# A TensorE order written out by hand while the modulation comes in by quarters, in a one-core diffusion block

## The chip, the cores and the metric

The kernel runs on one core of one Trainium2 chip. The metric is the device time of one execution in microseconds (us). Three runs of the kernel before took 872.28, 872.78 and 876.59 us, with a median of 872.78 us.

## What is computed

One layer on 1024 latent tokens and 256 context tokens of width 1024. What matters here is its beginning:

```
shift, scale, gate = split(silu(c) @ w_ada + b_ada, 3)       # c: 1024, w_ada: 1024 x 3072
h  = rmsnorm(x, g_pre) * (1 + scale) + shift                  # 1024 x 1024
hc = rmsnorm(ctx, g_pre) * (1 + scale_c) + shift_c            # 256 x 1024, from c_ctx
na_q, na_k, na_v, na_z, g_qkv, g_z, g_b, g_a = split(h @ w_in)   # w_in: 1024 x 4112
...
x + gate * rmsnorm(concat([o_na * silu(na_z), o_g * silu(g_z)]) @ w_out, g_post)
```

Neighbourhood attention and a bidirectional gated delta rule follow; they fill the rest of the time and are not touched.

## The kernel before, in words

The code in question is `phase0`, the first 110 us or so. The features of h are its 1024 input channels, in eight slices of 128 (k = 0 to 7) that stand on the partitions. Everything is needed as a pair of fp32r tiles, a high part and the rest: `hh` and `hl` for h, `wh` and `wl` for weights. A product is then three matmuls: hh with wh, hl with wh, hh with wl.

**Shift and scale by quarters.** `ada(q)` (line 287) handles slices 2q and 2q+1. It loads four pieces of w_ada of 512 KB (tiles `wada`, seven buffers), multiplies each with two matmuls of 32 columns (`par`, line 294), and loads and splits two groups of weights (`wr_nv`, `wr_qk`: a cast on ScalarE at line 448, a subtraction on GpSimd at line 449). Then VectorE copies the sums (`rows`, line 306), four small matmuls turn them (`pa`, line 310), VectorE makes `ab` and `am` (lines 314 and 315), and `modulate` (line 255) makes hh and hl of both slices: VectorE at line 259, ScalarE at line 265, VectorE at line 266.

**Products of a quarter.** `products(q)` (line 323) adds slices 2q and 2q+1 to six sums in PSUM for the first 512 tokens (group 0): `pv` of four token tiles (24 matmuls of 264 columns) and `pq`, `pk` (12 matmuls of 512 columns). The code calls `ada(q)` and then `products(q-1)` (lines 353 to 356).

**Group 1.** The other 512 tokens come as rows (`xra`, four loads), whose squares ScalarE sums (line 337), and transposed (`xta`, four loads into the same four buffers, so each waits for a square). The norms go through GpSimd, VectorE, a transpose on TensorE (`prr`, line 245) and a copy on ScalarE (`rbb`, line 246). Two gate products for group 0 (`pz`, 24 matmuls of 512 columns each, with the weights `wg1536` and `wg3584`) are called between the groups.

**What sets the order.** All loads are issued on SyncE's queue (SP) in the order of the code (`chain`), each one after the buffer that it fills is free; the raw weights `wr` have three buffers. The order on the five engines is set by the framework's scheduler, which puts an instruction where its own timing model finds it ready. A hand-made edge (`order`) ties one instruction behind another on its engine without a wait on the chip. Before the change there is one such edge for TensorE in this stage: the first `pq` matmul of products(2) stands behind the last `pa` matmul of quarter 3 (`self.after`, lines 328 and 464). `pe` (line 594), used later in the kernel, ties each TensorE instruction that it is given behind the one given before.

Of the kernel before, what the change touches and what calls it, by code (L numbers as in the profile page):

```python
# [20 lines left out]
P = 128  # L21
# [120 lines left out]
class K:  # L142
    def __init__(self, tc, I, out, dbg=None):
        self.tc, self.nc, self.I, self.out = tc, tc.nc, I, out
        self.dbg = dbg or {}
        self.na_first = None
        self.gm = {}
        self.gate = self.after = None

    def order(self, r, before):  # L150
        self.tc.add_manual_dep(r.ins, before, mybir.DependencyInfo(mybir.DependencyClass.NoSync,
                               mybir.DependencyReason.DATA), reason="order on a queue")

# [40 lines left out]
    def phase0(self):  # L194
# [10 lines left out]
        with tc.tile_pool(name="p0", bufs=1, side="right", reuse_waits="tile") as p0:  # L205
# [50 lines left out]
            def modulate(rw, hi, lo, k, w, rb, alt=True):  # L256
                m = hi.shape[-1]
                a, b = am[:, k, w:w + 1], ab[k // 2][:, 0, k % 2, w:w + 1]
                nc.vector.scalar_tensor_tensor(rw, rw, a, rb[:, :m], ALU.mult, ALU.mult)
                if k % 2 and alt:  # L260
                    nc.scalar.activation(rw, rw, AF.Identity, bias=b)
                    nc.scalar.copy(hi, rw)
                    nc.gpsimd.tensor_tensor(lo, rw, hi.bitcast(F32), ALU.subtract)
                else:
                    nc.scalar.activation(hi, rw, AF.Identity, bias=b)  # L265
                    nc.vector.scalar_tensor_tensor(lo, rw, b, hi.bitcast(F32), ALU.add, ALU.subtract)
# [18 lines left out]
            sels = []  # L285

            def ada(q):
                par = at(f"par{q}", "tb", 2)
                for k2 in range(0, KC, 2):
                    wa = p0.tile([P, 2, 2, 256], F32, name=f"wada{q}{k2}", tag="wada", bufs=7)  # L290
                    chain(wa, I["w_ada"][q][:, k2:k2 + 2])
                    for j in range(2):
                        g = 32 * ((k2 + j) % 4)
                        nc.tensor.matmul(par[g:g + 32, :], sc[:, k2 + j, :],
                                         wa[:, j, :, :].rearrange("p n c -> p (n c)"),
                                         start=(k2 < 4), stop=(k2 >= 4), tile_position=(0, g))
# [9 lines left out]
                nc.vector.tensor_copy(rows, par)  # L306
                pa = at(f"pa{q}", "tb", 2)[:, :8].rearrange("p (n c w) -> p n c w", n=2, c=2)
                for n in range(2):
                    for cc in range(2):
                        last = nc.tensor.matmul(pa[:, n, cc, :], rows[:, 256 * n + P * cc:256 * n + P * cc + P],  # L310
                                                self.sel, start=True, stop=True).ins.name
# [7 lines left out]
                sels.append(last)  # L319
# [3 lines left out]
            def products(q):  # L323
                ks = range(2 * q, 2 * q + 2)
                for t in g0:
                    self.mm_tok(pvs[t][:, :264], wv, 0, 264, self.nat_tok(t - 2), ks)
                for i in range(2):
                    if i == 0 and q + 1 in (3,):
                        self.after = sels[q + 1]
# [22 lines left out]

            for q in range(4):
                ada(q)
                if q:
                    products(q - 1)
# [9 lines left out]
            products(3)  # L366
# [67 lines left out]
    def load_w(self, pool, c0, n, tag, bufs=(3, 4, 4), halves=2, load=None, ks=None, dst=None):  # L434
# [5 lines left out]
        for k0 in [ks[0]] if ks else range(0, KC, kk):  # L440
# [7 lines left out]
            nc.scalar.copy(hi, raw)  # L448
# [6 lines left out]
    def mm_chan(self, ps, w, hh, hl, t0, n, perm=False, ks=range(KC)):  # L455
        nc = self.nc
        his, los = w
        for k in ks:
# [4 lines left out]
            r = nc.tensor.matmul(ps, wh, xh, start=(k == 0), stop=False)  # L463
            if self.after:
                self.order(r, self.after)
                self.after = None
            nc.tensor.matmul(ps, wh, xl, start=False, stop=False)  # L467
            nc.tensor.matmul(ps, wl, xh, start=False, stop=(k == KC - 1))  # L468

    def mm_tok(self, ps, w, c0, n, xsel, ks=range(KC)):  # L470
        nc = self.nc
        his, los = w
        for k in ks:
            wh, wl = his[k][:, c0:c0 + n], los[k][:, c0:c0 + n]
            xh, xl = xsel(k)
            nc.tensor.matmul(ps, xh, wh, start=(k == 0), stop=False)  # L476
            nc.tensor.matmul(ps, xl, wh, start=False, stop=False)  # L477
            nc.tensor.matmul(ps, xh, wl, start=False, stop=(k == KC - 1))  # L478
# [1078 lines left out]
```

## Time and profile before

| | us |
|---|---|
| median of three runs | 872.78 |
| the profiled execution | 871.71 |
| its span | 869.9 |
| TensorE busy in the span | 824.9 (95%) |
| VectorE, ScalarE, GpSimd busy | 502.7, 417.3, 357.3 |
| mean granted TensorE clock | 0.972 of 2.4 GHz |

A busy time is the sum in which an engine has an instruction under way. A share over the whole span mixes stages; the stage of the change is read from the timeline. "PEclk" is the clock that TensorE was granted, as a share of 2.4 GHz; 0.50 is 1.2 GHz. TensorE's matmuls overlap, so what one costs in a dense stretch is the distance from its start to the next one's start, which is shorter than the duration in the row.

### The profile page before, as it was taken

The numbers are of one execution on the slowest core, as the hardware profiler recorded it, in microseconds if no ns is written. First come the engines' busy times: TensorE is split into PE (matmuls) and PEld (weight loads), VectorE is DVE, ScalarE is ACT, GpSimd is POOL, SyncE is SP. The second block draws the span as 40 slices with busy tenths as digits, with TensorE's granted clock in tenths as the row PEclk, the third lists the DMA queues.
The fourth block names the chain that finished last, engine by engine and source line by source line (L and its number), as shares of the span: only waits on it lengthen the run. The fifth ranks groups of instructions, "written<-read, shape, count | busy, mean of one in ns | idle before, by whom it ended". The sixth has DMA issues, their size and how long they took to land.

```text
span 869.9 us, 16461 instructions
## 1 busy us (share of the span) xinstructions
PE 824.9 (95%) x6082; PEld 696.4 (80%) x6082; DVE 502.7 (58%) x1051; ACT 417.3 (48%) x1087; POOL 357.3 (41%) x430
## 2 busy tenths in 40 slices
PE   6999999999999989989898999899999999999996
PEld 3678887888788867769786788788898988878885
DVE  3444455536743699859935964456666655653342
ACT  5244334753664643355314334366666667734210
POOL 2224141453462553328262100655757559624110
PEclk9999999999999999989998999699999999999999
DMA  8778352255444825562597569995967925134251
GB/s 340 265 259 295 97 170 88 73 170 168 142 157 154 221 85 170 176 171 81 176 283 226 160 187 290 419 258 149 313 179 262 259 78 191 49 110 133 87 184 69
DMA packets 86054, 159.65 MB, mean 184 GB/s; under 512 B 18373, under 2 KB 45334, under 8 KB 83798
## 3 DMA queue, kind: packets, MB, share of 16 engines
q1 hardware_dynamic: 78486, 144.94, 53.0%
q10 hardware_dynamic: 7488, 13.67, 5.1%
q8 instruction: 48, 0.79, 0.4%
q14 instruction: 32, 0.26, 0.1%
HBM read 109.51 MB, written 52.42 MB: 186 GB/s over the span
## 4 chain that ended last, share of the span: by engine, by line
PE 59%; DVE 16%; DMA 15%; issue 4%; ACT 2%; POOL 2%; SPq 1%; DVEq 0%; POOLq 0%; ACTq 0%
PE py L1369 3%; PE py L1370 3%; PE py L1371 3%; DVE tb L1078 3%; DVE vb L1081 3%; PE pa L1260 2%; PE pz L463 2%; PE pz L468 2%; PE pz L467 2%; PE po L789 2%; DMA wada<-in_w_ada 2%; PE pa L1271 2%; PE po L784 2%; DMA pm_dram<-pm 2%; PE tr L772 2%
## 5 line engine op out<-in xcount | busy, mean ns | idle before, releaser
L759 ACT ACTIVATE pt<-pt,nm 128x544 f32<-128x544 f32 (+1 forms) x64 | 50.5, 790 | 37.5 <-DVE nm L758 37.0
L758 DVE CUSTOM_DVE_ANT_0 pt<-sc,gm 128x544 f32<-128x544 f32 (+1 forms) x64 | 49.4, 771 | 32.2 <-PE sc L754 25.8
L742 POOL TENSOR_TENSOR gm<-gt,mk 128x288 f32<-128x288 f32 (+1 forms) x48 | 46.5, 971 | 29.1 <-DVE nm L758 28.8
L1232 POOL TENSOR_SCALAR kd<-kt,kd 128x128 f32<-128x128 f32 x72 | 42.7, 605 | 20.5 <-PE pa L1271 19.9
L1020 ACT ACTIVATE em<-em,gc 128x128 f32<-128x128 f32 x80 | 25.5, 391 | 34.9 <-DMA em<-gc_dram 29.7
L467 PE MATMUL pz<-hl,wh_gz 128*128 128x512 f32 x96 | 38.6, 402 | 0.0
L463 PE MATMUL pz<-hh,wh_gz 128*128 128x512 f32 x96 | 38.3, 399 | 0.0
L468 PE MATMUL pz<-hh,wl_gz 128*128 128x512 f32 x96 | 38.2, 398 | 0.0
L476 PE MATMUL pv<-wh_nv,hh 128*128 128x264 f32 x128 | 35.5, 296 | 2.0 <-ACT hh L265 1.7
L477 PE MATMUL pv<-wh_nv,hl 128*128 128x264 f32 x128 | 36.8, 292 | 0.0
L1431 DVE TENSOR_TENSOR finv<-py,ggb 128x512 f32<-128x512 f32 x16 | 10.9, 689 | 43.2 <-ACT finv L1430 43.1
L478 PE MATMUL pv<-wl_nv,hh 128*128 128x264 f32 x128 | 35.6, 287 | 0.0
L1274 DVE SCALAR_TENSOR_TENSOR s<-s,egl,pa 128x128 f32<-128x128 f32 x64 | 19.6, 344 | 27.2 <-PE pa L1271 27.2
L1039 POOL TENSOR_SCALAR_AFFINE_SELECT qe<-qe 128x256 f32<-128x256 f32 x32 | 25.5, 800 | 24.1 <-DVE qe L1038 24.1
L887 DVE SCALAR_TENSOR_TENSOR acc_v<-xp_v,cols,acc_v 128x1282 f32<-128x1282 f32 x16 | 29.1, 1817 | 10.9 <-ACT acc_v L885 10.6
L1078 DVE TENSOR_TENSOR tb<-ab,vb 120x31 f32<-120x31 f32 (+15 forms) x62 | 30.2, 487 | 8.7 <-DMA ab<-ab_dram 7.1
L1137 POOL COPY tm<-ld 32x320 f32<-32x320 f32 x16 | 7.4, 464 | 65.0 <-DMA tm_dram<-tm 27.1
L1430 ACT ACTIVATE finv<-py 128x512 f32<-128x512 f32 x16 | 9.5, 597 | 48.6 <-PE py L1371 30.5
L1238 POOL TENSOR_SCALAR vb<-v,beta 128x128 f32<-128x128 f32 x40 | 24.2, 604 | 20.4 <-DVE y L1244 17.2
L772 PE MATMUL tr<-c,pt 128*96 128x128 f32 (+1 forms) x192 | 31.8, 275 | 0.0
L1035 DVE SCALAR_TENSOR_TENSOR pm<-pk,beta,em 128x128 f32<-128x128 f32 x80 | 23.5, 342 | 14.0 <-PE pk L1028 10.9
L770 ACT COPY tcx<-tc 128x256 f32<-128x256 f32 x64 | 23.4, 366 | 16.2 <-PE tc L768 15.8
(432 smaller groups left out, 2852.7 us busy)
## 6 DMA issues: line engine op xcount, KB each, us to landing
wada<-in_w_ada SPq DMA_DIRECT2D x16, 512.0 KB
em<-gc_dram SPq DMA_DIRECT2D x20, 256.0 KB
pm_dram<-pm SPq DMA_DIRECT2D x20, 256.0 KB
tm_dram<-tm SPq DMA_DIRECT2D x8, 640.0 KB
kk<-qk_dram SPq DMA_DIRECT2D x16, 320.0 KB
tm<-tm_dram SPq DMA_DIRECT2D x4, 1280.0 KB
kq_dram<-kq SPq DMA_DIRECT2D x4, 1152.0 KB
kq<-kq_dram SPq DMA_DIRECT2D x4, 1152.0 KB
```

What stands on the lines that cost most here:

```text
L463: r = nc.tensor.matmul(ps, wh, xh, start=(k == 0), stop=False)
L467: nc.tensor.matmul(ps, wh, xl, start=False, stop=False)
L468: nc.tensor.matmul(ps, wl, xh, start=False, stop=(k == KC - 1))
L476: nc.tensor.matmul(ps, xh, wh, start=(k == 0), stop=False)
L477: nc.tensor.matmul(ps, xl, wh, start=False, stop=False)
L478: nc.tensor.matmul(ps, xh, wl, start=False, stop=(k == KC - 1))
L742: r = nc.gpsimd.tensor_tensor(self.gm[hh][:, 384 - n:384].rearrange("p (n c r) -> p n c r", c=nco, r=4), gv, self.mk[:, mo:mo + n].rearran ...
L758: nc.vector.tensor_tensor_reduce(pt[:, 384 - n:], sc[:, 512 - n:768], gm[:, 384 - n:], -1.0, 3.0e38, ALU.add, ALU.min, nm)
L759: self.last_exp = nc.scalar.activation(pt[:, 384 - n:], pt[:, 384 - n:], AF.Exp, bias=nm, scale=-1.0, accum_out=sums[:, ct, hh:hh + 1]).in ...
L772: self.pe(nc.tensor.transpose(pl[:m, rc * P:(rc + 1) * P], pt[:, 384 + (rc - 3) * m:384 + (rc - 2) * m], self.ident))
L1078: nc.vector.tensor_tensor(t3, bc(ab[:, 0:m, m:m + 1], [r, m, n]), bc(vb[:, m:m + 1, m:], [r, m, n]), ALU.mult)
L1232: r = nc.gpsimd.tensor_scalar(kd[d], kt_[:, t, :], self.kd[:, h, d, t:t + 1], None, ALU.mult)
```

## The change

Every TensorE instruction issued between the start of quarter 0 and the end of products(2), and again in products(3), is tied behind the one before in the order of the code (`mm` calls `pe` while `seq` is set). `ada` and `products` become generators, so that the code can be interleaved: `ada(q)` stops after the copy `rows`, `products(q)` after two and after four token tiles. The order of the code in quarter q is then: pv of tiles 2 and 3 for quarter q-1; the eight `par` matmuls of quarter q; pv of tiles 4 and 5 for quarter q-1; `pa` of quarter q; pq and pk for quarter q-1. On ScalarE the weight casts of a quarter, and the squares in `load_rows`, are tied behind the last hh that was issued before them in the code.

```diff
+    def mm(self, *a, **k):
+        r = self.nc.tensor.matmul(*a, **k)
+        if self.seq:
+            self.pe(r)
...
-                    nc.scalar.activation(hi, rw, AF.Identity, bias=b)
+                    self.last_hh = nc.scalar.activation(hi, rw, AF.Identity, bias=b).ins.name
...
                 rows = p0.tile([P, 512], F32, name=f"rows{q}", tag="rows", bufs=1)
                 nc.vector.tensor_copy(rows, par)
+                yield
                 pa = at(f"pa{q}", "tb", 2)[:, :8].rearrange("p (n c w) -> p n c w", n=2, c=2)
...
             def products(q):
                 ks = range(2 * q, 2 * q + 2)
                 for t in g0:
                     self.mm_tok(pvs[t][:, :264], wv, 0, 264, self.nat_tok(t - 2), ks)
+                    if t % 2:
+                        yield
                 for i in range(2):
-                    if i == 0 and q + 1 in (3,):
-                        self.after = sels[q + 1]
                     self.mm_qk(pqk[i], wqk[i], i, 0, ks)
...
-                    nc.scalar.activation(x, x, AF.Square, accum_out=ss[:, i:i + 1])
+                    self.order(nc.scalar.activation(x, x, AF.Square, accum_out=ss[:, i:i + 1]), self.last_hh)
...
+            self.seq = True
+            before = iter(())
             for q in range(4):
-                ada(q)
-                if q:
-                    products(q - 1)
+                a = ada(q)
+                for g in (before, a, before, a, before):
+                    next(g, None)
+                before = products(q)
+            self.seq = False
...
-            products(3)
+            self.seq = True
+            for _ in before:
+                pass
+            self.seq = False
...
-            nc.scalar.copy(hi, raw)
+            r = nc.scalar.copy(hi, raw)
+            if self.seq and self.last_hh:
+                self.order(r, self.last_hh)
```

The matmuls of `ada`, `mm_chan` and `mm_tok` go through `self.mm`; `self.after` and `sels` are gone. No instruction is added, removed or resized. The built programs differ in order on all engines within the first 440 of TensorE's instructions, and nowhere after.

The first place is TensorE around the `par` matmuls of quarter 1 (`par1<-wada10` to `wada16`; `pv2_1` to `pv5_1` are the four token tiles, `wh_nv10_0` the weights of slices 0 and 1). Before:

```order
L310 MATMUL pa0_250<-c128_60,rows0_248 128x2 x4
L294 MATMUL par1_264<-wada10_265,sc_129 32x512 x2
L476 MATMUL pv2_1_204<-wh_nv10_0_228,hh_112 128x264
L476 MATMUL pv3_1_205<-wh_nv10_0_228,hh_112 128x264
L476 MATMUL pv4_1_206<-wh_nv10_0_228,hh_112 128x264
L476 MATMUL pv5_1_207<-wh_nv10_0_228,hh_112 128x264
L463 MATMUL pq0_0_208<-hh_112,wqk_h_202 128x512
L463 MATMUL pk0_0_209<-hh_112,wqk_h_202 128x512
L294 MATMUL par1_264<-wada12_269,sc_129 32x512 x2
```

After, from the end of the pv matmuls of tiles 2 and 3:

```order
L157 MATMUL pv3_1_205<-wh_nv10_0_228,hl_113 128x264
L157 MATMUL pv3_1_205<-wl_nv10_0_229,hh_112 128x264
L157 MATMUL par1_276<-wada10_277,sc_129 32x512 x2
L157 MATMUL par1_276<-wada12_281,sc_129 32x512 x2
L157 MATMUL par1_276<-wada14_285,sc_129 32x512 x2
L157 MATMUL par1_276<-wada16_289,sc_129 32x512 x2
L157 MATMUL pv4_1_206<-wh_nv10_0_228,hh_112 128x264
L157 MATMUL pv4_1_206<-wh_nv10_0_228,hl_113 128x264
```

Before, the four pairs of quarter 1 stand apart, the first ahead of any product and the others among them; now they stand in a row behind the twelve matmuls of tiles 2 and 3.

The second place is ScalarE at the modulation of quarter 3 (`hh<-raw,ab3`). Before:

```order
L448 CAST wg1536h_501<-wr_gz15360_0_503 128x512
L448 CAST wg1536h_501<-wr_gz15364_4_507 128x512
L337 ACTIVATE xra0_513,ss4__511<-xra0_513 128x1024
L337 ACTIVATE xra1_516,ss4__511<-xra1_516 128x1024
L265 ACTIVATE hh_112<-raw_135,ab3_456 128x512 x2
L337 ACTIVATE xra2_519,ss4__511<-xra2_519 128x1024
L337 ACTIVATE xra3_522,ss4__511<-xra3_522 128x1024
```

After:

```order
L461 CAST wg1536h_501<-wr_gz15360_0_503 128x512
L461 CAST wg1536h_501<-wr_gz15364_4_507 128x512
L272 ACTIVATE hh_112<-raw_135,ab3_480 128x512 x2
L342 ACTIVATE xra0_513,ss4__511<-xra0_513 128x1024
L342 ACTIVATE xra1_516,ss4__511<-xra1_516 128x1024
L342 ACTIVATE xra2_519,ss4__511<-xra2_519 128x1024
L342 ACTIVATE xra3_522,ss4__511<-xra3_522 128x1024
```

Two squares of group 1 went behind the modulation. The casts of the quarters stood behind the hh of the quarter ahead in both.

The third place is ScalarE just after that, from the copy of the last pv sum (`vt5`) on; `wg3584h` are the gate weights of `pz4`, `rbb` the norms of group 1, `xta0` its slices 0 and 1, `xrc0` context rows. Before:

```order
L499 COPY vt5_1_616<-pv5_1_207 128x248
L246 COPY rbb_553<-prr6_559 128x512
L265 ACTIVATE hh_112<-xta0_525,ab0_255 128x512
L448 CAST wg3584h_533<-wr_gz35840_0_535 128x512
L261 ACTIVATE xta0_525<-xta0_525,ab0_255 128x512
L448 CAST wg3584h_533<-wr_gz35844_4_539 128x512
```

After:

```order
L511 COPY vt5_1_616<-pv5_1_207 128x248
L459 DMA wr_gq0_0_1092<-in_w_in 128x512
L461 CAST wg3584h_533<-wr_gz35840_0_535 128x512
L461 CAST wg3584h_533<-wr_gz35844_4_539 128x512
L539 ACTIVATE sh_q00_621<-pq0_0_208 128x512
L253 COPY rbb_553<-prr6_559 128x512
L459 DMA wr_gq0_4_1098<-in_w_in 128x512
L539 ACTIVATE sh_k00_627<-pk0_0_209 128x512
L459 DMA wr_gk0_0_1167<-in_w_in 128x512
L342 ACTIVATE xrc0_543,ss2__512<-xrc0_543 128x1024
L272 ACTIVATE hh_112<-xta0_525,ab0_255 128x512
```

`rbb` and the first hh of group 1 stood ahead of the two gate casts and now stand behind them. On TensorE the transposes `prr6`, which feed `rbb`, moved from ahead of the 24 matmuls of `pz0` to behind 19 of them, and the first pv of group 1 from among the matmuls of `pz4` to behind them.

## Rows read from the trace of the kernel before

**Rows 1.** Busy time by window: stretch, length, PE, PEld, DVE, ACT, POOL, PEclk, DMA, GB/s.

```profile
59.38:94.70 35.32, 35.05 (x200) 30.58 (x199) 15.65 (x21) 14.53 (x27) 10.83 (x8) 1.00 0.65 222
...
19.30:26.00 6.70, 5.99 (x19) 2.65 (x16) 2.89 (x5) 2.64 (x4) 2.11 (x3) 0.50 1.04 413
```

**Rows 2.** Timeline of TensorE at 21: start, us, engine line operation, [idle before].

```profile
21.04 1.25 PE L476 MATMUL pv<-wh_nv,hh 128*128 128x264 f32 x4 [0.71 <-ACT hh L265]
```

**Rows 3.** Timeline of TensorE, 26 to 60.

```profile
26.38 0.28 PE L478 MATMUL pv<-wl_nv,hh 128*128 128x264 f32 x1
26.50 0.28 PE L476 MATMUL pv<-wh_nv,hh 128*128 128x264 f32 x1
...
26.98 0.40 PE L467 MATMUL pq<-hl,wqk_h 128*128 128x512 f32 x1
27.21 0.40 PE L468 MATMUL pq<-hh,wqk_l 128*128 128x512 f32 x1
...
29.68 1.05 PE L294 MATMUL par<-wada,sc 128*32 128x512 f32 x4
...
32.66 0.95 PE L310 MATMUL pa<-c,rows 128*128 128x2 f32 x8
33.53 1.92 PE L294 MATMUL par<-wada,sc 128*32 128x512 f32 x16
...
53.55 0.75 PE L476 MATMUL pv<-wh_nv,hh 128*128 128x264 f32 x4 [0.94 <-ACT hh L265]
...
59.38 0.60 PE L245 MATMUL prr<-c,rr 128*128 128x128 f32 x4
```

**Rows 4.** Timeline of VectorE, at the modulation of quarter 1 and of group 1.

```profile
34.04 1.42 DVE L259 SCALAR_TENSOR_TENSOR raw<-raw,am,rba 128x512 f32<-128x512 f32 x2
...
60.64 7.48 DVE L259 SCALAR_TENSOR_TENSOR xta<-xta,am,rbb 128x512 f32<-128x512 f32 x8 [1.35 <-ACT rbb L246]
```

**Rows 5.** Timeline of ScalarE, 40 to 70.

```profile
40.68 1.39 ACT L265 ACTIVATE hh<-raw,ab 128x512 fp32r<-128x512 f32 x2 [3.42 <-DVE raw L259]
...
50.45 1.06 ACT L337 ACTIVATE xra<-xra 128x1024 f32<-128x1024 f32 x1 [3.25 <-DMA xra<-in_x]
...
51.74 1.06 ACT L337 ACTIVATE xra<-xra 128x1024 f32<-128x1024 f32 x1
...
52.80 1.32 ACT L265 ACTIVATE hh<-raw,ab 128x512 fp32r<-128x512 f32 x2
...
56.01 0.19 ACT L337 ACTIVATION_READ_ACCUMULATOR xra<-xra 128x1 f32 x1
...
60.02 0.59 ACT L246 COPY rbb<-prr 128x512 f32<-128x512 f32 x1 [0.94 <-PE prr L245]
...
63.70 0.62 ACT L448 CAST wg3584h<-wr_gz 128x512 fp32r<-128x512 f32 x1 [1.55 <-DMA wr_gz<-in_w_in]
...
64.85 0.61 ACT L448 CAST wg3584h<-wr_gz 128x512 fp32r<-128x512 f32 x1
...
68.82 1.05 ACT L337 ACTIVATE xrc<-xrc 128x1024 f32<-128x1024 f32 x1
```

**Rows 6.** Timeline of GpSimd, 64 to 68.

```profile
64.40 3.17 POOL L449 TENSOR_TENSOR wg3584l<-wr_gz,wg3584h 128x512 fp32r<-128x512 f32 x2 [6.75 <-DMA wr_gz<-in_w_in]
```

**Rows 7.** Timeline of SP's queue: DMA issues, 44 to 58.

```profile
44.44 1.88 SPq L156 DMA_DIRECT2D xra<-in_x  x4
...
56.64 0.92 SPq L156 DMA_DIRECT2D wr_gz<-in_w_in  x2
```

**Rows 8.** TensorE's timeline where it had waited longest in the span's middle.

```profile
319.93 1.12 PE L909 MATMUL tp<-c,acc_k 128*128 128x128 f32 x4 [3.26 <-ACT sq L915]
...
417.09 0.41 PE L944 MATMUL tb<-c,tok 128*128 128x128 f32 x2 [2.86 <-DVE tok L921]
```

**Rows 9.** Busy time by window, just behind those two waits.

```profile
319.70:322.90 3.20, 2.98 (x10) 2.48 (x11) 3.17 (x3) 3.04 (x16) 2.44 (x4) 0.50 0.18 68
...
417.20:424.00 6.80, 6.80 (x58) 6.80 (x58) 6.80 (x17) 2.91 (x7) 1.19 (x1) 1.00 0.49 157
```

More of the change, by code (lines that the diff above doesn't have):

```diff
@@ L147, in __init__ @@
         self.gm = {}
-        self.gate = self.after = None
+        self.gate = self.last_pe = self.last_hh = None
+        self.seq = False
     def order(self, r, before):
@@ L283, in phase0 @@
             pqk = [at(f"p{c}0_0", "ta", 3) for c in "qk"]
-            sels = []
             def ada(q):
@@ L293, in ada @@
                         g = 32 * ((k2 + j) % 4)
-                        nc.tensor.matmul(par[g:g + 32, :], sc[:, k2 + j, :],
-                                         wa[:, j, :, :].rearrange("p n c -> p (n c)"),
-                                         start=(k2 < 4), stop=(k2 >= 4), tile_position=(0, g))
+                        self.mm(par[g:g + 32, :], sc[:, k2 + j, :],
+                                wa[:, j, :, :].rearrange("p n c -> p (n c)"),
+                                start=(k2 < 4), stop=(k2 >= 4), tile_position=(0, g))
                 ks = range(2 * q, 2 * q + 2)
@@ L309, in ada @@
                     for cc in range(2):
-                        last = nc.tensor.matmul(pa[:, n, cc, :], rows[:, 256 * n + P * cc:256 * n + P * cc + P],
-                                                self.sel, start=True, stop=True).ins.name
+                        self.mm(pa[:, n, cc, :], rows[:, 256 * n + P * cc:256 * n + P * cc + P], self.sel,
+                                start=True, stop=True)
                 abh = p0.tile([P, 2, 2, 2], F32, name=f"ab{q}")
@@ L318, in ada @@
                 ab.append(abh)
-                sels.append(last)
                 for k in ks:
@@ L365, in phase0 @@
             norms(g1, rb2, ss1)
-            products(3)
+            self.seq = True
+            for _ in before:
+                pass
+            self.seq = False
             for t in g0:
@@ L462, in mm_chan @@
                 xh, xl = (v.rearrange("p (a t c) -> p t a c", a=8, t=4) for v in (xh, xl))
[L463 to L468, printed above, removed]
+            self.mm(ps, wh, xh, start=(k == 0), stop=False)
+            self.mm(ps, wh, xl, start=False, stop=False)
+            self.mm(ps, wl, xh, start=False, stop=(k == KC - 1))
     def mm_tok(self, ps, w, c0, n, xsel, ks=range(KC)):
@@ L475, in mm_tok @@
             xh, xl = xsel(k)
-            nc.tensor.matmul(ps, xh, wh, start=(k == 0), stop=False)
-            nc.tensor.matmul(ps, xl, wh, start=False, stop=False)
-            nc.tensor.matmul(ps, xh, wl, start=False, stop=(k == KC - 1))
+            self.mm(ps, xh, wh, start=(k == 0), stop=False)
+            self.mm(ps, xl, wh, start=False, stop=False)
+            self.mm(ps, xh, wl, start=False, stop=(k == KC - 1))
     def nat_tok(self, t):
```

## The prediction

> **What bounds the kernel now.** I read the page first: TensorE is busy for 95% of the span, so whatever shortens or lengthens TensorE's own sequence shows in the end. Then the busy time by window: from 59.4 to 94.7 us TensorE idles for 0.27 us in all [rows 1], and the page's slices behind it stay as full for a long time. A shift of TensorE at 60 us therefore reaches the end unless something behind it soaks it up. The reader should see the converse as well: an idle stretch that the change opens there is paid in full. Third, TensorE's timeline from 21 us, where the first product can start [rows 2], to 59.38, where the transposes for group 1 end this stage [rows 3]. In it the clock is half until 26.0 [rows 1], quarters' `par` pieces stand among the products, and the last modulation is waited for. Fourth, the timelines of ScalarE, VectorE, GpSimd and SP, for what group 1 waits for.
>
> **Prices.** In dense full-clock stretches a pv matmul costs 0.12 us from start to start and a pq, pk or pz matmul 0.235 [rows 3]. Two `par` matmuls alone (four records) cost 1.05, while eight in a row (sixteen records) cost 1.92 [rows 3]; `pa` costs 0.9. At half clock I double these.
>
> **The first stage, on TensorE.** Up to `pa` of quarter 0 nothing moves. The first hh is there at 21.04 as before [rows 2], since its chain has no changed part. From there, in the new order:
>
> - pv of tiles 2 and 3, quarter 0: the second matmul waits for hl, one VectorE pass of 0.71 later (half of 1.42, [rows 4]), then eleven at 0.24: 24.4.
> - `par` of quarter 1: 3.84 at half clock, of which 1.6 fit before 26.0; the other 58% at full clock take 1.1: 27.1.
> - pv of tiles 4 and 5 (12 x 0.12), `pa` 0.9, pq and pk (12 x 0.235): 5.2 together: 32.3.
> - quarters 2 and 3 each: 24 pv 2.9, `par` 1.92, `pa` 0.9, pq and pk 2.8, so 8.5: 49.3, with 0.3 for waits on hl 49.6.
> - products(3): 2.9 and 2.8: 55.3.
>
> Before, the same point is 59.38 [rows 3]. The gain is 4.1: some 2.5 from pairs of `par` that no longer stand alone (six such pieces before, of which the first lay in a pause and is paid now), 0.94 from the wait before products(3) [rows 3], the rest from short waits. What hides the modulation: from the end of `pa`, 0.4 to the first pass of VectorE, two passes of 0.7, two hh of 0.7 one behind, so the first hh is there 1.8 and the second 2.6 after `pa`; pq and pk of the quarter before cover 2.8. If VectorE is slowed by GpSimd, up to 0.5 a quarter shows. The loads keep up: the last `wada` of a quarter waits for a buffer that now frees earlier, except quarter 2's, which waits for the first `par` of quarter 1 and is still issued some 7 us before it is used.
>
> **The casts.** ScalarE's casts of the quarters stood behind the same hh before, so this part of the change costs and gives nothing. The two squares that went behind hh of quarter 3 free it of a delay of 0.5 [rows 5].
>
> **What sets group 1's loads.** The second wg1536 load waits for a buffer that GpSimd frees after the cast behind hh of quarter 2, and the four `xra` loads stand behind it on SP [rows 7]. That hh ended at 42.07 [rows 5]. Now `pa` of quarter 2 ends at 38.1, hh at 40.7, so `xra` is issued 1.35 earlier and its first load lands at 49.1 instead of 50.43. Hh of quarter 3 ends at 46.8 + 2.6 = 49.4; the squares follow, 1.29 each [rows 5], until 54.6 instead of 56.2: 1.6 earlier. The `xta` loads wait for the squares, the wg3584 loads stand behind `xta` on SP. Their first cast began 7.06 after their issue [rows 5, 7]; issued at 55.0, it begins at 62.05 and ends at 62.7.
>
> **The second stage, where it is given back.** TensorE is 4.1 earlier, the wg3584 weights only 1.6.
>
> - 55.3: pz0 and the transposes, 24 x 0.235 + 0.3: 61.2. Then pz4 needs the cast: **idle 1.45**. Two matmuls, then the low part of the weights, which GpSimd makes 1.58 after the cast (half of 3.17, [rows 6]): 64.25, **idle 1.1**. The other 22: 69.4. Before, pz4 stood later than its weights.
> - ScalarE: the second cast comes 1.15 after the first [rows 5] and ends at 63.8, then a copy of pq and `rbb`, 0.6 each [rows 5]: 65.0 instead of 60.6. VectorE's eight passes over `xta`, 0.71 each where the loads are there (7.48 before, as it waited for some, [rows 4]), end at 70.8; the first hl of group 1 at 71.6. TensorE needs it at 69.9, after three matmuls with hh: **idle 1.7**.
> - ScalarE's square of `xrc` (68.82 before [rows 5]; its load stands behind wg3584 on SP, so 67.2 now) is ahead of the first hh: 69.1, in time. The second hh comes after two more hh, a square, two biases and its own cast, 4.7 later: 73.8. TensorE needs it at 72.5: **idle 1.3**.
> - From there hh and hl run ahead of TensorE.
>
> Idle time 5.55, against 0.27 before: 5.3 lost. The sum is 5.3 - 4.1 = **+1.2 us**.
>
> **Bounds.** The first stage: a wait of 0.5 in each quarter leaves a gain of 2.5; none at all, 4.4. The second: if the weights come no earlier than before (cast at 63.70), all its stalls grow by 1.65 at their head and 7.2 is lost; if they come before 61.2, the gate waits fall away and some 1 to 2 of the others remain. So +4.7 to -3.4, by these rows.
>
> The load's price can be weighed against a rule. The Trainium skill, DMA: Bandwidth & Descriptors, section Anatomy of one DMA, fits 2.0 us and bytes at 436 GB/s for one DMA of the software queue, an estimate of 2.6 us for these 256 KB. The trace disagrees for this place with its 7.06, because four `xta` loads are ahead. By the rule the weights would be there at 57.6 and the sum would be that of the second rival. I take the row, since the same four loads are ahead after the change.
>
> **Rivals.**
>
> 1. *The clock falls in the second stage: slower.* Four waits of 1.1 to 1.7 stand within 12 us of a stretch that has had none. A wait of 3.26 was followed by a granted clock of 0.50 for at least 3.2 us, one of 2.86 by full clock [rows 8, 9], so the profile leaves it open for shorter waits close together; the start of this very stage, with TensorE idling 0.7 here and there, ran at half clock for 6.7 us [rows 1, 2]. It decides if the drop comes behind the last wait: half of 3.2 to 6.7 us is lost, 1.6 to 3.4, and the total is +2.8 to +4.6 (a drop between the waits costs nothing, as the later waits shrink by it). [...]
> 2. *The gain is kept: faster.* The wg3584 loads arrive before TensorE, as the loads of 50 to 60 us are spread less by the squares between them. Then pz4 never waits, `rbb` is 4 earlier, and -2.3 to -4.4 remains: about 869.7, at the edge of what can be told. Against it: the load waits for the last square, which depends on hh of quarter 3 and on `xra`, and only 1.6 comes from that side.
> 3. *Nothing moves.* TensorE's order before might be as good as written out, because loads and not order pace it. Against it: the last `par` pair of quarter 1 ran at 29.68 with no idle time ahead of it [rows 3], so order put it there and no load. The time would be the old one, 872.8.
>
> **How the numbers follow.** The sum is made against the profiled execution, 871.71 (span 869.9 and 1.8 around it): 872.9. That execution is 1.07 under the median of the three runs, 872.78, so I forecast the median at 872.78 + 1.2 = **874.0**. A difference of 0.5% (4.4 us) is about the least that can be told from no change here; that is 868.4 and 877.1. The forecast (no clock drop, within the bounds) gets 0.52, of which 0.03 lie over 877.1; rival 1 gets 0.24 and half of it is over; rival 2 gets 0.16 and half of it is under 868.4; rival 3 gets 0.08. So faster 0.08, same 0.77, slower 0.15. The range leaves out the ends of both rivals: 868.8 to 878.2, the upper end being a clock drop on top of a first stage that gains 3 instead of 4.
>
> **What would show it.** Right: products(3) ends near 55.3 with `par` in four rows of about 2 us; the last square ends near 54.6; TensorE waits for wg3584's cast and low part just after 61, then for hl and hh of group 1 near 70 and 73; the end of group 1 lies some 1 us later than 94.5. Wrong: products(3) not before 58, or no idle time between 60 and 75, or a granted clock of 0.50 after 60, or a later stage that starts with a shift and ends without it.

## The result and the profile after

| | before | changed |
|---|---|---|
| median of 20 runs each, same chip | 872.00 us | 876.28 us |
| ratio | | 1.0042 [1.0025, 1.0060] |
| the profiled execution (span) | 871.71 (869.9) | 875.39 (873.7) |
| TensorE busy in the span | 824.9 (95%) | 821.3 (94%) |
| mean granted TensorE clock | 0.972 | 0.974 |

The change costs 3.7 us by the ratio (0.0042 x 872), with an interval of 2.2 to 5.2; the two medians stand 4.3 apart. That lies inside the band of 0.5% for most of its interval and inside the range; the forecast was +1.2.

The same windows as in [rows 1], of the changed kernel:

```profile
19.30:26.00 6.70, 5.05 (x24) 3.20 (x28) 2.73 (x4) 2.64 (x4) 2.28 (x2) 0.50 1.02 410
59.38:94.70 35.32, 32.09 (x183) 26.95 (x182) 20.94 (x30) 18.60 (x39) 13.44 (x12) 1.00 0.68 229
```

TensorE, which had 0.27 us without work between 59.38 and 94.70, now has 35.32 - 32.09 = 3.23, at full clock. TensorE's timeline shows what came ahead of that and where the 3.23 lie (it answers to [rows 2, 3]):

```profile
20.75 0.59 PE L157 MATMUL pv<-wh_nv,hh 128*128 128x264 f32 x1 [2.69 <-ACT hh L272]
...
24.27 2.83 PE L157 MATMUL par<-wada,sc 128*32 128x512 f32 x16
...
32.25 0.28 PE L157 MATMUL pv<-wh_nv,hh 128*128 128x264 f32 x1
...
32.67 0.28 PE L157 MATMUL pv<-wh_nv,hh 128*128 128x264 f32 x1
32.98 0.39 PE L157 MATMUL pv<-wh_nv,hl 128*128 128x264 f32 x1
...
34.15 1.92 PE L157 MATMUL par<-wada,sc 128*32 128x512 f32 x16
36.00 0.39 PE L157 MATMUL pv<-wh_nv,hh 128*128 128x264 f32 x1
...
37.56 0.95 PE L157 MATMUL pa<-c,rows 128*128 128x2 f32 x8
...
50.44 0.39 PE L157 MATMUL pv<-wh_nv,hh 128*128 128x264 f32 x1
51.23 0.39 PE L157 MATMUL pv<-wh_nv,hl 128*128 128x264 f32 x1 [0.40 <-DVE hl L273]
...
57.22 0.39 PE L157 MATMUL pz<-hh,wg1536h 128*128 128x512 f32 x1
...
62.94 0.40 PE L157 MATMUL pz<-hh,wg1536l 128*128 128x512 f32 x1
64.48 0.50 PE L157 MATMUL pz<-hh,wg3584h 128*128 128x512 f32 x1 [1.15 <-ACT wg3584h L461]
...
65.84 0.50 PE L157 MATMUL pz<-hh,wg3584l 128*128 128x512 f32 x1 [0.63 <-POOL wg3584l L464]
...
72.94 0.39 PE L157 MATMUL pv<-wh_nv,hl 128*128 128x264 f32 x1 [1.30 <-DVE hl L273]
...
74.32 0.51 PE L157 MATMUL pv<-wh_nv,hh 128*128 128x264 f32 x2 [0.15 <-ACT hh L269]
```

The first hh is there at 20.75, the `par` pieces stand in whole rows of sixteen records, and the first stage ends at 57.22 instead of 59.38. Then come the four waits 1.15, 0.63, 1.30 and 0.15. ScalarE and SP tell why (they answer to [rows 5, 7]):

```profile
50.95 1.04 ACT L342 ACTIVATE xra<-xra 128x1024 f32<-128x1024 f32 x1
...
55.03 0.18 ACT L342 ACTIVATION_READ_ACCUMULATOR xra<-xra 128x1 f32 x1
...
63.81 1.27 ACT L461 CAST wg3584h<-wr_gz 128x512 fp32r<-128x512 f32 x2 [7.56 <-DMA wr_gz<-in_w_in]
...
65.47 0.58 ACT L253 COPY rbb<-prr 128x512 f32<-128x512 f32 x1
...
73.66 0.60 ACT L269 CAST hh<-xta 128x512 fp32r<-128x512 f32 x1
```

```profile
43.49 2.83 SPq L163 DMA_DIRECT2D xra<-in_x  x4
52.12 3.45 SPq L163 DMA_DIRECT2D xta<-in_xt  x4
55.66 1.93 SPq L163 DMA_DIRECT2D wr_gz<-in_w_in  x2
```

The loads of wg3584 are issued 0.98 earlier than before (55.66 against 56.64), and their cast begins 0.11 later (63.81 against 63.70). TensorE gained 2.16 and the weights nothing, so the gain is waited away, and `rbb`, behind the two casts, comes 5.45 later than before.

What answers to [rows 8, 9] are these waits of TensorE behind 316 us, and the windows at them:

```profile
320.81 0.66 PE L921 MATMUL tp<-c,acc_k 128*128 128x128 f32 x4 [2.46 <-ACT sq L927]
...
336.21 0.41 PE L956 MATMUL tb<-c,tok 128*128 128x128 f32 x2 [3.55 <-DVE tok L933]
```

```profile
336.00:340.00 4.00, 3.79 (x11) 3.04 (x12) 4.00 (x9) 0.96 (x2) 0.00 (x0) 0.60 0.81 250
319.70:322.90 3.20, 1.71 (x9) 1.18 (x10) 3.13 (x6) 3.04 (x15) 1.62 (x2) 1.00 0.22 82
```

The wait near 320 is shorter than before and leaves the clock at 1.00 where it was 0.50, and one of 3.55 at 336 is followed by 0.60. By such stretches the shift (defined in the next section) swings between 320 and 415 us from -1.5 to +3.7.

### The profile page after: what moved, and what is told of

Read it like the earlier page. It is cut to its first block, busy times and chain, and to the rows that moved or that the text cites. A ratio compares the mean times of both kernels' runs of the same rounds, so it can differ in the third digit from the quotient of the medians.

```text
span 873.7 us, 16458 instructions
## 1 busy us (share of the span) xinstructions
PE 821.3 (94%) x6082; PEld 695.9 (80%) x6082; DVE 502.6 (58%) x1051; ACT 418.0 (48%) x1087; POOL 356.0 (41%) x430
## 4 chain that ended last, share of the span: by engine, by line
PE 62%; DVE 16%; DMA 12%; ACT 3%; issue 3%; SPq 1%; POOL 1%; DVEq 0%; POOLq 0%; ACTq 0%
PE pz L157 5%; PE pv L157 4%; PE gpl_k L157 4%; PE gpl_q L157 4%; PE py L1381 3%; PE py L1382 3%; PE py L1383 3%; PE pq L157 3%; DMA pm_dram<-pm 3%; PE gpl_v L157 3%; PE pa L1272 3%; DVE tb L1090 2%; PE po L801 2%; DVE vb L1093 2%; PE pa L1283 2%
## 5 line engine op out<-in xcount | busy, mean ns | idle before, releaser
L157 PE MATMUL pv<-wh_nv,hh 128*128 128x264 f32 x128 | 37.5, 298 | 4.1 <-ACT hh L272 2.7
L157 PEld LDWEIGHTS pv<-wh_nv,hh 128*128 128x128 f32 x128 | 24.7, 193 | 8.6 <-ACT hh L272 3.2
```

The source lines that it names most:

```text
L157: r = self.nc.tensor.matmul(*a, **k)
```

## The experiments

The scheduler also orders the rest of the kernel, so a run is read at several places. The shift is the start of the same matmul minus its start in the first profile of before, as a median over the matmuls of a stretch of 10 us; one profile each. Ahead of it stands the start of VectorE's modulation of quarter 1 (`raw<-raw`, the first row of [rows 4]) with the granted clock of 19.3 to 26.0 us. Up to there TensorE has the same order in all kernels that are before with an edit behind it, and likewise in all that are the change with an edit, so a difference of this start within a group is not the work of another order on TensorE. The runs with a clock of 0.75 or 0.81 have a lead of 0.7 to 2.2 us over 34.04 or 29.97, except change_again; before_again and keep have 0.6.

| run | quarter 1, us (clock) | shift at 58 us | 95 | 300 | 490 | 580 | end | ratio to before, 95% |
|---|---|---|---|---|---|---|---|---|
| before | 34.04 (0.50) | 0 | 0 | 0 | 0 | 0 | 0 | |
| the change | 29.97 (0.50) | -2.6 | +1.7 | +1.7 | +4.3 | +4.0 | +3.8 | 1.0042 [1.0025, 1.0060] |
| change_again | 29.97 (0.75) | -2.5 | +1.3 | +1.2 | -1.9 | -0.8 | -0.9 | 1.0059 [1.0033, 1.0084] |
| before_again | 33.48 (0.56) | -1.0 | -0.7 | -0.7 | -0.2 | -0.8 | -1.0 | 0.9996 [0.9971, 1.0021] |
| pe_only | 28.81 (0.75) | +0.2 | -0.4 | -0.5 | -1.8 | +0.1 | +1.2 | 1.0066 [1.0041, 1.0092] |
| act_only | 32.79 (0.75) | -1.7 | +3.0 | +3.0 | +2.0 | +4.3 | +6.0 | 1.0095 [1.0071, 1.0119] |
| early_wg | 30.30 (0.56) | -2.2 | +0.8 | +0.7 | -1.7 | +1.1 | +0.9 | 1.0045 [1.0024, 1.0066] |
| delay | 34.22 (0.53) | -0.3 | -0.4 | +1.1 | +0.7 | +2.6 | +3.8 | 1.0057 [1.0037, 1.0078] |
| other_block | 33.95 (0.51) | -0.6 | -0.7 | -0.3 | +1.0 | +2.6 | +3.8 | 1.0071 [1.0044, 1.0097] |
| change_other_block | 29.23 (0.75) | -3.2 | +1.3 | +1.5 | +2.9 | +7.4 | +8.8 | 1.0089 [1.0060, 1.0117] |
| keep | 29.38 (0.56) | -2.2 | -1.8 | -1.9 | -3.5 | +1.9 | +3.1 | 1.0045 [1.0023, 1.0068] |
| bufs5 | 32.89 (0.75) | -1.5 | -2.0 | -2.1 | -2.8 | -3.0 | -3.1 | 0.9987 [0.9962, 1.0012] |
| bufs6 | 33.84 (0.51) | -0.5 | -1.1 | -1.1 | +0.6 | -0.4 | +0.6 | 0.9979 [0.9953, 1.0004] |
| rows4 | 31.86 (0.81) | -2.4 | -3.0 | -3.0 | -4.0 | -3.6 | -1.1 | 1.0005 [0.9985, 1.0026] |

**pe_only: the change without ScalarE's ties.** TensorE's written order stays.

```diff
-                    self.order(nc.scalar.activation(x, x, AF.Square, accum_out=ss[:, i:i + 1]), self.last_hh)
+                    nc.scalar.activation(x, x, AF.Square, accum_out=ss[:, i:i + 1])
...
-            if self.seq and self.last_hh:
-                self.order(r, self.last_hh)
```

> TensorE's written-out order alone; the casts and squares on ScalarE are not tied to the modulation. Theory (the order gains some 2 us in the first stage; the ties turn ScalarE's order of the second stage round, so that the copy rbb stands behind the wg3584 casts, and this gives the gain back): products(3) ends 1.5 to 2.1 earlier than before's 59.38, TensorE still waits some 1 to 2 us for wg3584 near 61 to 65, but no longer for hl and hh of group 1 near 73; TensorE stands within 0.5 of before at 150 us, and the time is within 1 us of before. Rival A (the loads set the second stage whatever ScalarE's order): waits for hl near 73 as in the change, +1.7 at 150 us. Rival B (the order gains nothing lasting and is itself the loss): +1.5 or more at 150 us with few waits.

Measured, from ScalarE's timeline of this kernel:

```profile
38.90 0.64 ACT L461 CAST wh_nv<-wr_nv 128x528 fp32r<-128x528 f32 x1 [6.87 <-DMA wr_nv<-in_w_in]
39.44 0.72 ACT L272 ACTIVATE hh<-raw,ab 128x512 fp32r<-128x512 f32 x1
...
59.15 0.62 ACT L461 CAST wg3584h<-wr_gz 128x512 fp32r<-128x512 f32 x1 [0.45 <-DMA wr_gz<-in_w_in]
```

Without the ties the cast of wg3584 comes at 59.15, 4.66 earlier than in the change (1.16 of it is the lead at quarter 1), and TensorE waits for nothing between 58 and 95. TensorE's timeline and the windows around its stall show the other side:

```profile
41.53 0.39 PE L157 MATMUL pv<-wh_nv,hl 128*128 128x264 f32 x1 [0.93 <-DVE hl L273]
...
43.21 0.39 PE L157 MATMUL pv<-wh_nv,hl 128*128 128x264 f32 x1 [1.05 <-DVE hl L273]
...
60.03 0.39 PE L157 MATMUL pz<-hh,wg1536h 128*128 128x512 f32 x1
```

```profile
40.60:44.40 3.80, 1.82 (x14) 1.46 (x15) 2.56 (x2) 1.82 (x4) 3.80 (x4) 1.00 0.64 208
44.40:47.90 3.50, 3.50 (x17) 0.58 (x16) 0.00 (x0) 2.30 (x4) 1.13 (x1) 0.51 1.00 394
```

Here TensorE waits for hl of quarter 2, and the clock is 0.51 behind it, over a `par` row that takes 3.60 instead of 1.92. The first stage therefore ends at 60.03, no earlier than before. Why hl is late is seen on VectorE:

```profile
40.19 2.97 DVE L273 SCALAR_TENSOR_TENSOR hl<-raw,ab,hh 128x512 fp32r<-128x512 f32 x2 [0.97 <-ACT hh L272]
```

A cast now stands ahead of the first hh of quarter 2 (38.90; in the change it comes at 41.02, behind both hh), and GpSimd, whose subtractions follow the casts, is busy for all 3.80 us of the first window. The two passes for hl take 2.97 beside it, against 1.42 in the change. So the ties keep the first stage short, and the same ties hold back group 1's loads: the casts delay the second wg1536 load and with it `xra` (43.49 against 41.33 here, of which 1.16 is the lead), and the squares, tied behind hh of quarter 3, delay `xta` and wg3584. The shift of -0.5 at 300 us is what the theory told, but by luck: the first stage did not gain, TensorE did not wait for wg3584, and the lead of 1.16 is in it. The median was 6 us over before's and not within 1.

**act_only: the kernel before with the ties alone.**

```diff
+                    self.last_hh = nc.scalar.activation(hi, rw, AF.Identity, bias=b).ins.name
...
+                    self.order(nc.scalar.activation(x, x, AF.Square, accum_out=ss[:, i:i + 1]), self.last_hh)
...
+            if self.seq and self.last_hh:
+                self.order(r, self.last_hh)
```

> The kernel before with only the ScalarE ties (casts and squares behind the modulation). Theory: products(3) ends no more than 0.6 earlier than before; the second stage takes the order of the changed kernel, rbb stands behind the wg3584 casts at about 65.5, eight VectorE passes follow and the first hl of group 1 comes near 72.5, while TensorE is through with pz4 near 69.5: a wait of 2 to 3 us for hl, TensorE +2 to +3 at 150 us. Rival A (loads alone): no wait for wg3584, since TensorE comes to it at 64 as before, and no loss: within 0.5 at 150 us. Rival B (TensorE's order is the loss): -0.5 to 0 at 150 us.

TensorE's timeline of this kernel:

```profile
65.82 0.50 PE L468 MATMUL pz<-hh,wg3584h 128*128 128x512 f32 x1 [2.02 <-ACT wg3584h L451]
...
67.17 0.50 PE L473 MATMUL pz<-hh,wg3584l 128*128 128x512 f32 x1 [0.62 <-POOL wg3584l L454]
...
74.27 0.39 PE L482 MATMUL pv<-wh_nv,hl 128*128 128x264 f32 x1 [1.29 <-DVE hl L267]
```

The waits of the change are all there without its order on TensorE: 2.02, 0.62 and 1.29 against 1.15, 0.63 and 1.30. The shift at 300 us is +3.0, more than the change's +1.7, though this run had a lead of 1.25 at quarter 1; from there to 300 us it loses 4.2. The second stage's loss thus comes from the ties, and the written order pays some of it back. The theory's +2 to +3 held; the waits for wg3584, which it did not tell, are the larger part of it.

**early_wg: the change with wg3584's loads ahead of `xta`.**

```diff
+            gates.append(self.gate_proj(vp, ps, 4, 3584, gate_w(3584)))
             xr = load_t(I["xt"], "a", "x", 4, 2)
-            gates.append(self.gate_proj(vp, ps, 4, 3584, gate_w(3584)))
```

> The changed kernel with the two wg3584 loads ahead of the xta loads on SP. Theory: they are issued near 52 to 53 and land by 58, pz4 does not wait, rbb no longer stands behind them, and the stage keeps its gain: TensorE at 150 us 1.5 to 2.2 earlier than before (3.2 to 3.9 earlier than the change). Rival A (the loads set the stage): xta, 1.7 later, is now what TensorE waits for near 70, and the gain over the change stays under 1.5. Rival C (clock): a granted clock of 0.5 between 60 and 95 in any of these runs.

The cast comes at 55.83 and the two gate waits are gone, but ScalarE and TensorE show a new one:

```profile
63.80 1.06 ACT L342 ACTIVATE xrc<-xrc 128x1024 f32<-128x1024 f32 x1 [6.05 <-DMA xrc<-in_cx]
64.86 0.57 ACT L253 COPY rbb<-prr 128x512 f32<-128x512 f32 x1
```

```profile
71.57 0.39 PE L157 MATMUL pv<-wh_nv,hl 128*128 128x264 f32 x1 [2.03 <-DVE hl L273]
```

`rbb` now stands behind a square that waits 6.05 for a load, so it came only 0.61 earlier than in the change, and hl is waited for by 2.03 (the next hl, GpSimd's, by 0.48). The shift at 300 us is +0.7 where the theory had -1.5 to -2.2, so the earlier weights were worth 0.5 (against change_again) to 1.0.

**keep: early_wg, and `rbb` freed.** The loads of the context are called behind group 1's norms, their squares tied behind `rbb`, and `prr` stands ahead of the first gate product.

```diff
-                nc.scalar.copy(rb, pt[:, :n * P])
+                self.last_hh = nc.scalar.copy(rb, pt[:, :n * P]).ins.name
...
+            rb2 = rbt("b")
+            norms(g1, rb2, ss1)
             load_rows(I["cx"], "c", ssc, "wada", 7)
             xc = load_t(I["cxt"], "c", "wada", 7, 4)
...
+            self.hold = self.last_tr
             for g in gates:
```

> The changed kernel with the second stage set right: wg3584 loaded ahead of xta, the transposes prr6 ahead of pz0 (its first matmul tied behind them), and the squares of xrc tied behind rbb. Theory: no wait of TensorE over 0.5 between 57 and 95 us, and the 2 us of the first stage are kept: 1.6 to 2.3 earlier than before at 150 and at 300 us. The end is not the test, as the scheduler interleaves the small matmuls behind 500 us in a third way here; if that costs what the others do, the time is within 2 us of before. Rival (loads): TensorE waits 1 to 2.5 for xta, hh or hl near 66 to 75, and is no more than 0.5 ahead at 150 us.

ScalarE's timeline, TensorE's wait near 57, and the window of the second stage:

```profile
58.29 0.59 ACT L257 COPY rbb<-prr 128x512 f32<-128x512 f32 x1 [1.71 <-PE prr L256]
```

```profile
57.63 0.63 PE L256 MATMUL prr<-c,rr 128*128 128x128 f32 x4 [0.97 <-DVE gates L523]
```

```profile
59.38:94.70 35.32, 35.21 (x199) 30.57 (x198) 12.83 (x25) 14.54 (x29) 6.63 (x6) 1.00 0.62 210
```

TensorE idles 0.11 in the second stage, and the shift at 300 us is -1.9, against 0 and -0.7 in the two profiles of before: a gain of 1.2 to 1.9. From 58 to 300 us it loses 0.3, where the change loses 4.3. So what took the gain was the order of the loads and of `rbb`, as act_only and early_wg said. One wait over 0.5 is left, against the expectation: with `prr` ahead of the gates, TensorE waits 0.97 for the norms just ahead of that stage. The median is still 0.45% above before, and between 490 and 580 us the shift goes from -3.5 to +1.9. That is another effect, which the next runs measure.

**delay, other_block, change_other_block: matmuls added.** Seven matmuls (delay) or two (the others; the last with the change) are added ahead of a gate product of group 1, near 95 us. They write a sum that the real ones start anew.

```diff
+        for _ in range(again):
+            nc.tensor.matmul(ps, his[0], hh[:, 0, t0:t0 + n], start=True, stop=True)
...
-            self.mm_chan(pz, w, self.hh, self.hl, 512 * gr, 512)
+            self.mm_chan(pz, w, self.hh, self.hl, 512 * gr, 512, again=7 if (j, gr) == (0, 1) else 0)
```

> The kernel before with seven more matmuls of 0.235 us ahead of the first matmul of pz0 of group 1 (its first product computed eight times), so a pure delay of 1.64 us near 95 us and nothing else in that part. If the second half of the change's loss (+1.7 at 300 us, +3.8 at the end) follows from the delay itself through the waits for VectorE behind 320 us: +1.6 at 300 us and +3 to +4 at the end, as in the change. If it is scatter of the stretch behind 320 us: +1.6 at 300 us and +1 to +2.5 at the end, the median over the rounds near +1.6. If the stretch absorbs delays: under +0.8 at the end.

> The kernel before with two more matmuls of 0.235 us ahead of pz0 of group 1 (its first product three times). That is enough for the scheduler to interleave the small matmuls tz and tu with pk and pz otherwise between 500 and 545 us, word for word as in the runs with the order alone and the ties alone; it is those runs' proper yardstick. If that other interleaving is what made them 4 us longer at the end than at 300 us: +0.5 at 300 us, +2 to +3 between 500 and 570 us, +2.5 to +5 at the end. If it costs nothing: +0.5 at the end, and the 4 us of those runs come from the stretch of 320 to 480 us.

> The changed kernel with the same two matmuls, and so with the same interleaving behind 500 us as the run before. Read against that run: if the loss of the second stage is passed on one for one, it is 1.7 slower at 300 us and 1.2 to 2.2 slower at the end; if the stretch behind 320 us enlarges a delay, 3 to 4.5 slower at the end; if it absorbs it, under 1.

By the price of 0.235 the additions are 1.6 and 0.47, and that is what the shift shows there (+1.5 and +0.4 between 95 and 300). Yet two matmuls cost 6.2 us in the medians (0.0071 x 871). Up to 490 us the trace has +1.0, then it goes to +2.6 and +3.8. The window of 530 to 575 of before and then of other_block:

```profile
530.00:575.00 45.00, 40.59 (x546) 35.78 (x544) 19.06 (x48) 22.05 (x58) 20.78 (x35) 0.81 0.94 350
```

```profile
530.00:575.00 45.00, 42.40 (x516) 37.52 (x515) 17.57 (x45) 19.08 (x49) 18.61 (x31) 0.73 0.91 331
```

The granted clock there is 0.73 instead of 0.81 and fewer matmuls fit in. What differs is the order: with other_block's edit the scheduler puts a block of 120 small matmuls (`tu`, at 503 us) two `pk` matmuls later than before, and later blocks shift likewise. Before, the change, the two repeats, bufs5, bufs6 and rows4 share one such interleaving (0.81 each); the other seven have others, with 0.73, early_wg 0.77. From 490 to 580 us the shift of the first group changes by -1.0 to +1.1, that of the seven grows by 1.6 to 5.4. So the medians of pe_only, act_only, early_wg, keep and delay hold some microseconds that go with the other late order and not with what their edits do in the first 100 us, and for these only the traces up to 300 us are read.

change_other_block against other_block compares the change on equal terms: +1.8 at 300 us, and 878.31 against 876.31, +2.0, in the medians. That fits a cost that is passed on one for one. It does not settle it: five and six executions spread over 3.2 and 5.0 us, and the two profiles end 5.0 apart.

In this run the clock did fall in the second stage. TensorE's waits and the windows behind them:

```profile
63.84 0.50 PE L157 MATMUL pz<-hh,wg3584h 128*128 128x512 f32 x1 [1.06 <-ACT wg3584h L461]
...
65.20 0.61 PE L157 MATMUL pz<-hh,wg3584l 128*128 128x512 f32 x1 [0.63 <-POOL wg3584l L464]
```

```profile
65.60:69.00 3.40, 3.40 (x10) 2.67 (x9) 3.40 (x6) 1.90 (x4) 0.79 (x1) 0.52 1.01 370
69.00:94.70 25.70, 25.64 (x157) 22.48 (x156) 17.41 (x27) 15.13 (x33) 11.18 (x10) 1.00 0.57 200
```

The clock is 0.52 from 65.6 to 69.0, and the wait for hl, 1.30 in the change, is gone. From 58 to 95 us, ahead of the added matmuls, this run loses 4.4 (-3.2 to +1.3), the change 4.4 as well (-2.6 to +1.7): the drop added nothing.

**change_again and before_again: the same two kernels once more.**

> The changed kernel once more, unchanged. The shift at 300 us should repeat (+1.5 to +1.9), being order and loads. If what is added behind 320 us follows from the shift, it repeats as well: +3.3 to +4.3 at the end in the profile and in the median. If it is scatter, the profile ends anywhere from +1 to +5 and the median settles near +1.7.

> The kernel before once more, unchanged: how far two profiles of one program differ. If the stretch behind 320 us scatters from run to run (as the two of the change did, +2.1 and -2.1 there), this one differs from the first by up to 2 us behind 320 us and by under 0.8 at 300 us, and its median is within 1 us of the shared one.

The change has +1.2 at 300 us this time, before -0.7: a difference of 1.9, as in the first pair (1.7). Behind 300 us one profile of the change adds 2.1 and the other takes off 2.1, so two profiles of one program end 4.7 apart. The ratio is 1.0059, near the first. Neither branch of what was expected fits: the profile ends at -0.9 and the median 4.3 above before's. before_again came as expected (-0.7 at 300 us, its median 0.2 under the shared one).

**bufs5, bufs6, rows4: a delay of the first stage with before's late interleaving.** The aim was a delay of 1 to 3 us that leaves the late block as it is. bufs5 sets the count of these buffers to five, here and at their three other uses, bufs6 to six.

```diff
-                    wa = p0.tile([P, 2, 2, 256], F32, name=f"wada{q}{k2}", tag="wada", bufs=7)
+                    wa = p0.tile([P, 2, 2, 256], F32, name=f"wada{q}{k2}", tag="wada", bufs=5)
```

```diff
-                nc.vector.tensor_copy(rows, par)
+                for _ in range(4 if q == 3 else 1):
+                    nc.vector.tensor_copy(rows, par)
```

> The kernel before with five buffers of wada instead of seven: the loads of the quarters come later, and with them the first stage, while the interleaving of the small matmuls behind 500 us stays word for word that of before. So it is a delay near the start without that side effect; I expect +1 to +4 at 300 us. If the stretch behind 320 us passes a delay on one for one, the median is above the shared one by the shift at 300 us, within 1.2; if it enlarges every delay as in the change (+1.4 at 300 us, median +4.2), it is 2 to 3 above that.

> The same with six buffers: a smaller delay, +0.2 to +2 at 300 us, same interleaving as before. One for one: the median above the shared one by the shift at 300 us, within 1.2. Enlarged: 2 to 3 us more than that, even for a shift under 1.

> The kernel before with the copy of quarter 3's par to rows done four times over: 1.8 to 2.1 us more on VectorE ahead of the last modulation, for which TensorE waits, and otherwise the same order on every engine but for single neighbours, word for word the same behind 100 us. So it is a delay of 1.5 to 2.5 us in the first stage (up to 4 if the granted clock falls behind that wait) with the interleaving of before behind 500 us. If the stretch behind 320 us passes a delay on one for one: the median stands above the shared one by the shift at 300 us (against both profiles of before, mean -0.35), within 1.2. If it enlarges a delay as the change's median suggests (shift 1.75, median 4.2): 2 to 3 us more than its shift.

None gave a delay. With fewer buffers the traces have shifts of -2.1 and -1.1, of which 1.15 and 0.20 are the lead at quarter 1, and the medians cannot be told from before's. In rows4 the four copies took their time on VectorE,

```profile
45.14 2.87 DVE L307 COPY rows<-par 128x512 f32<-128x512 f32 x4 [4.46 <-PE par L294]
```

while TensorE had products(2) to do. Most of its shift of -3.0 has another source, the stretch near 20 us; 2.18 of it stand already at quarter 1 (31.86 against 34.04):

```profile
19.30:26.00 6.70, 6.24 (x30) 3.81 (x30) 2.49 (x4) 2.64 (x4) 2.57 (x2) 0.81 1.04 414
```

The clock was 0.81 here, against 0.50 in the first profile of before, with the same order of TensorE up to there. Whether such a delay is paid one for one at the end was not shown by these three.

## Why the prediction was right or wrong

**Where TensorE gives back what it gains: right in kind.** The order of the waits (cast, low part, hl, hh) came as told, in the places told, and the sum up to 300 us is +1.7 in the first pair and +1.9 in the second, against the forecast +1.2. Two terms were mis-sized and partly cancel: the first stage gained less, and the second lost less. In part they must: behind a wait TensorE starts when the awaited tile is there, whatever it had gained before.

**The first stage: the gain of 4.1 was 2.16.** Quarter 0 went as told: the first `par` row ends at 27.10 (told 27.1), the next quarter begins at 32.25 (32.3). The term that was too small is the 0.3 for waits on hl. Quarters 2 and 3 took 18.2 together (32.25 to 50.44) where 17.0 was told, products(3) 6.8 instead of 5.7 (50.44 to 57.22). In each of them TensorE stops short of the first matmul that needs the second slice's hl. In quarter 2 that matmul starts at 32.98, 0.31 behind the one ahead of it and not 0.12, and VectorE ends this hl at 31.51 + 1.42 = 32.93:

```profile
31.51 1.42 DVE L273 SCALAR_TENSOR_TENSOR hl<-raw,ab,hh 128x512 fp32r<-128x512 f32 x2
```

The profile lists no idle time for such a stop, as the duration of the matmul ahead covers it. With the slower matmul behind it (0.23 for 0.12) each stop costs 0.3, in quarters 2 and 3 alike. products(3) has one more, for the first hl, with 0.40 of idle time (50.44 to 51.23, 0.67 over the spacing), and quarter 3 loses 0.2 ahead of it, waiting for hh. Together this is 1.9 of the 2.3 that the first stage took beyond its prices. The rest is small change, such as twelve pv behind a `par` row, which took 1.56 (36.00 to 37.56) and not 1.44.

**The modulation under GpSimd.** "Up to 0.5 a quarter" was a bound and came once, in VectorE's and GpSimd's timelines, where [rows 4] have 1.42:

```profile
47.97 2.33 DVE L266 SCALAR_TENSOR_TENSOR raw<-raw,am,rba 128x512 f32<-128x512 f32 x2
```

```profile
47.77 1.31 POOL L464 TENSOR_TENSOR wg1536l<-wr_gz,wg1536h 128x512 fp32r<-128x512 f32 x1 [2.21 <-DVE ab L320]
```

The two passes took 0.91 longer beside GpSimd's subtraction for the second wg1536. That delayed hh and hl of quarter 3, and to it belong the waits ahead of 50.44 and 51.23. pe_only has the same in quarter 2, with 2.97.

**"The casts cost and give nothing": right against before, but not the whole.** act_only, before with the ties, issues `xra` at 43.20, 1.24 ahead of before, and its lead at quarter 1 is 1.25. The change beat before's 44.44 by 0.95 (1.35 was told), as its hh of quarter 2 came 0.4 later than told (41.12 for 40.7). What the sentence left out is what the written order would do without the ties: pe_only issues `xra` 2.16 earlier than the change, 1.0 of it beyond its lead, and pays for it in the modulation.

**The load of the weights.** The last square ended at 55.2 (told 54.6) and the issue came at 55.66 (55.0), but the first cast began 8.15 after it, not 7.06: the weights landed as late as before. That was the lower bound of the text ("no earlier than before"). The step that failed is the price of 7.06, taken as fixed "since the same four loads are ahead". They stand closer together: before, two squares ran ahead of hh of quarter 3 and the `xta` loads, which wait for the squares, were issued over 4.92 us,

```profile
51.63 4.92 SPq L156 DMA_DIRECT2D xta<-in_xt  x4
```

while in the change all four squares follow that hh, and the loads come 0.49 later and within 3.45. In the four runs with 3.45 (the change, change_again, act_only, change_other_block) the price is 7.7 to 8.2, in the eight with 4.9 to 5.7 (the kernels without the ties) 5.9 to 7.2. The Trainium skill, DMA: Bandwidth & Descriptors, section Anatomy of one DMA, gives by its fit for the software queue an estimate of 2.6 us for 256 KB. The trace has 8.15 for a load that the profile puts on a queue called hardware_dynamic, behind four others, so the fit does not carry over. The second rival, which that estimate would have meant, did not happen.

**The second stage: 5.3 lost was told, 3.8 was measured.** TensorE came to the gates 1.9 later than told (57.22 for 55.3) and the weights 1.8 later (63.81 for 62.05), so the waits at the gates are near what was told: 1.15 and 0.63 for 1.45 and 1.1. The wait for hl was 1.30 for 1.7. Half of the difference is the last one, 0.15 for 1.3: the second hh was there at 74.26 (73.66 + 0.60), 0.5 later than told, but TensorE came to it 1.5 later than told, at 74.0 instead of 72.5. That makes 3.23 in place of 5.55. What TensorE lost is still more than its idle time. From 57.22 to 95 us the shift goes from -2.16 to +1.7, by 3.8, for 2.96 more idle time. Each wait costs 0.16 beyond its idle time: the matmul at 62.94 would have been followed at 63.17 by the spacing of 0.235, the next began at 64.48, which is 1.31 for an idle time of 1.15. Four waits make 0.65; the other 0.2 were not traced.

**Rival 1 (the clock falls).** In the change's profile it did not. In change_other_block it did, ahead of the later waits, and cost nothing, as the text had it for that place: waits of 1.06 and 0.63 were followed by 0.52 there, waits of 1.15 and 0.63 by 1.00 in the change. The Trainium skill, TensorE: Matmul & The Clock Gate, section Loop structure matters more than you think, has TensorE go cold where a long wait for a DMA stands between every two matmuls; no run here has that pattern, and it does not decide between these two. **Rival 2** needed the weights earlier; keep shows that most of the gain could be kept, by another order of the loads and of `rbb`. **Rival 3** fails: the first stage moved by 2.16.

**What stays open.** The ratios of the medians say +3.7 and, for change_again, +5.1 (0.0059 x 871); the traces up to 300 us say 1.7 and 1.9. The lower ends of the two intervals, 2.2 and 2.9, come near the latter. The other 2 us or so arise behind 320 us, in stretches that differ from run to run, in a kernel whose late order is that of before. What sets them was not found; no run with a pure delay and that late order came about. The prediction let the shift pass to the end unchanged and set the upper end of its range by a drop of the clock, which did not come, so that the range holds the median, 876.28, is in part luck. Its sign "a later stage that starts with a shift and ends without it" did come once, in change_again's profile (+1.2 at 300 us, -1.9 at 490).

## What to carry to other kernels

Where an engine is made faster in one stage, ask which load the next stage waits for and what frees its buffer: here the ties that kept the first stage's gain of 2.2 held the next one's weights, and the order of the loads and of one copy decided whether the gain stayed. A scheduler that orders the whole program can change a far block after a small edit: look at the order and the clock of the blocks that an edit doesn't touch before a difference in medians is put down to it. Compare one part's cost at the last point ahead of such blocks, and look first whether the two profiles stand alike ahead of the edit: here the clock near 20 us alone moved them by up to 2.2.

## What the runs showed of the hardware

- Waits of about the same length near the same place left the clock at 1.00 in one run (1.15, 0.63) and at 0.52 in another (1.06, 0.63); 0.93 and 1.05 in pe_only were followed by 0.51.
- Two VectorE passes took 2.33 instead of 1.42 beside one GpSimd subtraction of 1.31, and 2.97 in pe_only while GpSimd was busy throughout.
- The stretch of 19.3 to 26.0 ran at 0.50 in one run and at 0.81 in another with the same order on TensorE, and with that order the modulation of quarter 1 began 2.18 earlier (31.86 against 34.04); the lead was not lost up to 300 us (-3.0).
- 256 KB of weights landed and were cast 8.15 us after their issue behind four loads on SP that were issued within 3.45 us, and 7.06 us where the four were issued over 4.92: issued 0.98 earlier than before, they came no earlier.
